# Summing the squares of the first half of the tokens on TensorE instead of GpSimd

## The chip, the cores and the metric
The kernel runs on one core of one Trainium2 chip. The metric is the device time of one execution in microseconds (us). The core has engines with a queue of instructions each: TensorE (PE; its weight loads are listed as PEld), VectorE (DVE), ScalarE (ACT), GpSimd (POOL), and SyncE (SP), which here issues most of the transfers.

## The reference
The kernel is one inference step of a decoder layer for a prompt of 512 tokens and 8 samples of one token each, 520 tokens of width 1024. The layer is

```
x += W_out [ GatedDeltaNet heads (8 x 64) | NSA heads (8 x 64) ]( RMSNorm(x) @ W_in )
x += MemCrossAttn( RMSNorm(x), mem K/V )
x += relu( RMSNorm(x) @ W_up )^2 @ W_down

def rms_norm(x, gain):
    xf = x.astype(jnp.float32)
    y = xf * lax.rsqrt(jnp.mean(xf * xf, axis=-1, keepdims=True) + RMS_EPS)
    return (y * gain.astype(jnp.float32)).astype(x.dtype)
```

followed by a final norm. The change concerns the first of these norms: the mean of the squares of a token's 1024 values, for the product with W_in.

## The kernel before
**Layout.** The tokens lie feature-major: 1024 features as 8 chunks c of 128 partitions, the tokens along the free dimension. They are held in two halves, h = 0 with 256 prompt tokens and h = 1 with the other 256 and the 8 samples, 264 columns.

**Products.** W_in comes in panels of 128 columns. `load` (L243) has SP transfer a panel into one of two buffers wraw, and `split` cuts it in two parts: ScalarE casts the high part whi (L235), and VectorE subtracts it to get the low part wlo (L236). The tokens are cut in the same way in `scaled`: xh by ScalarE or VectorE in turn (L323, L321), xl by VectorE (L324). A product is then three products per chunk, whi with xh, whi with xl, wlo with xh (`mm` is L194), 24 for a panel and a half. They are added up in one of two accumulators ps_g; the narrow panel "bag" (40 columns) uses ps_m. The two accumulators take turns, so a panel's half can begin once the one two places before it has been moved out.

**The norm.** The gain goes into xh and xl, and the factor 1/rms of a token, rstd, is multiplied in when an accumulator is moved out (`times_rstd`, L328, on VectorE). rstd comes from the sum of the squares over all 1024 features. For h = 1 ScalarE squares each chunk into sq (L396), and TensorE multiplies it by a 128 x 128 matrix of ones in fp32, adding up the 8 chunks in ps_t; so the sum stands on all partitions. For h = 0 the function `ssq` has ScalarE square the first chunk into the tile ssq (L297) and the others into sq (L300), GpSimd adds them up in ssq (L301), and one product with ones follows. `rstd` then has ScalarE do Ln (L310) and Exp (L311).

**Order of the panels.** `mixers` calls for bag and k0 together, k1, the decay matrices of the DeltaNet heads (`dn_decay`: tiles P, 32 operations of 128x128 on VectorE in L767 of its first call, with transfers P<-cumd by SP), then q0, q1, `dn_mats`, ck, k2 and so on. bt is the bag's result, ready for five transposes (L226) whose results lead to beta and decay of the heads (sg, gd, cum, ct); of a panel of kind q or k, `dn_tile` makes pre and cv, the convolution acc (L725, L727), its gate sgm, the norm and qk (L745), for k also kt (L756). kv is what `cmp_tile` moves out of ck's accumulator.

**What sets the order.** The kernel is written in a framework of tiles that is started with `TILE = dict(schedule_with_timeline_sim=True)` (L19). It orders the instructions of each engine by a simulation of its own of when they could run, not by their place in the source, and each engine then executes its list in that order. A change of one instruction can so change the order elsewhere.

Of the kernel before, what the change touches and what calls it, by code (L numbers as in the profile page):

```python
# [7 lines left out]
F32 = mybir.dt.float32  # L8
# [3 lines left out]
AF = mybir.ActivationFunctionType  # L12
# [169 lines left out]
class Build:  # L182
# [173 lines left out]
    def setup(self):  # L356
        nc, I, cp = self.nc, self.I, self.cp
        nc.scalar.preload_act_table_set("natural_log_exp_and_others")
        X = self.x = self.xp.tile([128, 8, 520], F32, tag="x", name="x")
        self.xh = [X[:, :, 0:256], X[:, :, 256:520]]  # L360
        small = self.small = cp.tile([128, S_COLS], F32, name="small")
        nc.sync.dma_start(small[:], I["small"])
        nc.sync.dma_start(self.xh[0][:, 0:2, :], I["xa"][:, 0:2, :])
        bag = self.load(I["w_bag"])
        for c in range(2, 8, 2):
            nc.sync.dma_start(self.xh[0][:, c:c + 2, :], I["xa"][:, c:c + 2, :])
        k0 = self.load(I["w_in"][0])
        for c in range(0, 8, 4):
            nc.sync.dma_start(self.xh[1][:, c:c + 4, :], I["xb"][:, c:c + 4, :])
        cst = self.cst = cp.tile([128, C_CAU], F32, name="cst")  # L370
        nc.sync.dma_start(cst[:], I["consts"][:, 0:C_CAU])
        cau = self.ap.tile([128, 128], F32, tag="qp", name="cau", bufs=1)
        nc.sync.dma_start(cau[:], I["consts"][:, C_CAU:C_COLS])
        self.ident = cst[:, C_ID:C_ID + 128]
        self.ones = cp.tile([128, 128], F32, name="ones")
        nc.vector.memset(self.ones[:], 1.0)
        self.eps = cp.tile([128, 2], F32, name="eps")
        nc.vector.memset(self.eps[:, 0:1], EPS)
        nc.vector.memset(self.eps[:, 1:2], 1.0)
        self.idb = cp.tile([128, 128], BF16, name="idb")  # L380
        nc.vector.tensor_copy(self.idb[:], cst[:, C_ID:C_ID + 128])
        self.caub = cp.tile([128, 128], BF16, name="caub")
        nc.vector.tensor_copy(self.caub[:], cau[:])

        self.xn, self.r, self.early = [], [], []
        for h in range(2):
            n = HN[h]
            acc = self.tp.tile([128, 264], F32, tag="ssq", name="ssq") if h == 0 else None
            hl = self.xhl(h)
            for c in range(8):  # L390
                self.scaled(self.xh[h][:, c, :], n, 0, c, hl, nc.vector if c % 2 else None)
                if (h, c) == (0, 1):
                    self.early.append(self.parts(bag))
                if h:
                    sq = self.tp.tile([128, 264], F32, tag="sq", name="sq", bufs=2)
                    nc.scalar.activation(sq[:, :n], self.xh[h][:, c, :], AF.Square)  # L396
                    if c == 0:
                        total = self.psum("t")
                    self.mm(total[:, :n], self.ones[:], sq[:, :n], c == 0, c == 7)
                else:  # L400
                    self.ssq(acc, c, self.xh[h][:, c, :], n)
            if h == 0:
                self.early.append(self.parts(k0))
            self.r.append(self.rstd(acc, n, total if h else None))
            self.xn.append(hl)


# [1420 lines left out]
```

## Time and profile before

| | |
|---|---|
| median of 3 runs | 978.94 us (977.99 to 979.73) |
| the profiled execution | 981.79 us, of it 979.9 us span |
| TensorE busy | 945.0 us, 96% |
| VectorE busy | 695.0 us, 71% |
| ScalarE busy | 481.4 us, 49% |
| GpSimd busy | 144.3 us, 15%; 44.1 us of it in 47 additions of L301 |

The span is the time from the first to the last instruction that the profiler recorded on the core; the profiled execution's own time is a little longer. Busy shares are means over the whole program. An operation's duration overlaps that of the next one on the same engine a little, so several in a row take less than the sum of their durations. The additions of L301 are those of this norm and of later ones.

### The profile page before, as it was taken

Reading aid. Unit: us, or ns where it says so; the run is one execution under the profiler, and the core shown is the slowest. Engines: PE = TensorE matmul, PEld = TensorE weight load, DVE = VectorE, ACT = ScalarE, POOL = GpSimd, SP = SyncE. Lnnn points to the kernel's source line nnn. Section 1 sums busy time; section 2 is a strip of 40 time slices with the busy share of each in tenths; the row PEclk is TensorE's granted clock in tenths of the full one; section 3 lists DMA queues with packets and bytes.
Section 4 is the critical chain, followed back from the end, with each engine's and each line's share of the span. In section 5 each row is a group of like instructions: output and inputs, shape, how many; then the busy total and the mean of one; then the engine's idle time right before and its main releaser. Section 6 shows DMA issues by size and latency. Waiting matters only on the chain.

```text
span 979.9 us, 20589 instructions
## 1 busy us (share of the span) xinstructions
PE 945.0 (96%) x8160; PEld 870.5 (89%) x8160; DVE 695.0 (71%) x1405; ACT 481.4 (49%) x1041; POOL 144.3 (15%) x209
## 2 busy tenths in 40 slices
PE   6999999999999998999999999999999999999995
PEld 5989898898878876789988889899999999999994
DVE  6698669898777769756566569798676766666433
ACT  4485304168665444354444456576544454455331
POOL 2101008612031134104100004100000000000020
PEclk9999999999999999999999999999999999999997
DMA  7344553122033553355465532123322232233303
GB/s 271 127 162 141 165 166 113 65 66 69 24 125 117 192 199 110 139 186 198 188 235 217 216 108 87 33 98 125 112 99 98 87 109 97 88 108 108 108 12 88
DMA packets 57000, 123.78 MB, mean 126 GB/s; under 512 B 7608, under 2 KB 23672, under 8 KB 54184
## 3 DMA queue, kind: packets, MB, share of 16 engines
q1 hardware_dynamic: 54696, 113.29, 33.6%
q0 software_dynamic: 2208, 9.17, 2.6%
q8 instruction: 64, 1.05, 0.4%
q14 instruction: 32, 0.26, 0.1%
HBM read 111.06 MB, written 13.47 MB: 127 GB/s over the span
## 4 chain that ended last, share of the span: by engine, by line
PE 84%; DVE 10%; DMA 2%; ACT 2%; issue 1%; SPq 0%; POOL 0%; DVEq 0%; ACTq 0%
PE ps_g L194 37%; PE ps_o L194 14%; PE ps_m L194 11%; PE ps_t L194 11%; PE ps_s L194 8%; PE ps_t L226 2%; DVE wlo L236 1%; DMA wraw<-in_w_in 1%; DVE nb L806 1%; DMA out_mk_o<-mk 1%; PE ps_m L226 1%; DVE st L821 1%; DVE Xd L823 1%; DVE x L1625 1%; DVE kp L1159 1%
## 5 line engine op out<-in xcount | busy, mean ns | idle before, releaser
L194 PE MATMUL ps_g<-xh,whi 128*128 128x264 f32 (+1 forms) x672 | 195.1, 291 | 3.6 <-DVE nq L441 1.5
L194 PE MATMUL ps_g<-xh,wlo 128*128 128x264 f32 (+1 forms) x672 | 192.2, 287 | 1.9 <-DVE wlo L236 1.9
L194 PE MATMUL ps_g<-xl,whi 128*128 128x264 f32 (+1 forms) x672 | 194.0, 289 | 0.0
L194 PEld LDWEIGHTS ps_g<-xh,whi 128*128 128x128 f32 x672 | 127.7, 190 | 9.7 <-issue 5.1
L194 PEld LDWEIGHTS ps_g<-xh,wlo 128*128 128x128 f32 x672 | 127.5, 190 | 4.6 <-DVE wlo L236 2.3
L194 PEld LDWEIGHTS ps_g<-xl,whi 128*128 128x128 f32 x672 | 128.0, 190 | 2.6 <-issue 1.2
L301 POOL TENSOR_TENSOR ssq<-ssq,sq 128x256 f32<-128x256 f32 (+2 forms) x47 | 44.1, 938 | 513.7 <-ACT sq L300 513.4
L235 ACT CAST whi<-wraw 128x1024 fp32r<-128x1024 f32 (+1 forms) x67 | 69.4, 1037 | 95.0 <-PE ps_g L194 47.6
L235 ACT CAST wh<-wr 128x512 fp32r<-128x512 f32 x112 | 68.9, 620 | 67.4 <-PE ps_g L194 28.2
L236 DVE TENSOR_TENSOR wlo<-wraw,whi 128x1024 fp32r<-128x1024 f32 (+1 forms) x67 | 84.6, 1264 | 23.5 <-ACT whi L235 23.0
L236 DVE TENSOR_TENSOR wl<-wr,wh 128x512 fp32r<-128x512 f32 x112 | 76.3, 687 | 28.7 <-ACT wh L235 26.8
L194 PE MATMUL ps_g<-tyh,wl 128*128 128x260 f32 x256 | 72.3, 283 | 1.1 <-DVE wl L236 1.1
L194 PE MATMUL ps_g<-tyh,wh 128*128 128x260 f32 x256 | 72.6, 284 | 0.0
L194 PE MATMUL ps_g<-tyl,wh 128*128 128x260 f32 x256 | 72.5, 283 | 0.0
L194 PE MATMUL ps_o<-hh,wh 128*128 128x260 f32 x256 | 72.4, 283 | 0.0
L194 PE MATMUL ps_t<-hh,wh 128*128 128x260 f32 x256 | 72.4, 283 | 0.0
L194 PE MATMUL ps_t<-hh,wl 128*128 128x260 f32 x256 | 72.3, 283 | 0.0
L194 PE MATMUL ps_o<-hh,wl 128*128 128x260 f32 x256 | 72.3, 283 | 0.0
L194 PE MATMUL ps_o<-hl,wh 128*128 128x260 f32 x256 | 72.2, 282 | 0.0
L194 PE MATMUL ps_t<-hl,wh 128*128 128x260 f32 x256 | 72.1, 282 | 0.0
L235 ACT CAST wh<-ws 128x512 fp32r<-128x512 f32 x64 | 39.5, 617 | 48.7 <-PE ps_o L194 32.5
L236 DVE TENSOR_TENSOR wl<-ws,wh 128x512 fp32r<-128x512 f32 x64 | 43.7, 684 | 18.6 <-ACT wh L235 18.5
(466 smaller groups left out, 2539.2 us busy)
## 6 DMA issues: line engine op xcount, KB each, us to landing
wr<-in_w_up SPq DMA_DIRECT2D x64, 256.0 KB, 3.0
wr<-in_w_dn SPq DMA_DIRECT2D x64, 256.0 KB, 2.6
wraw<-in_w_in SPq DMA_DIRECT2D x26, 512.0 KB, 4.1
mK<-in_mkt SPq DMA_DIRECT2D x8, 1024.0 KB, 4.8
mK<-in_mv SPq DMA_DIRECT2D x8, 1024.0 KB, 6.9
w<-in_w SPq DMA_DIRECT2D x8, 512.0 KB, 3.5
wraw<-in_w_mk SPq DMA_DIRECT2D x8, 512.0 KB, 4.0
wraw<-in_w_mv SPq DMA_DIRECT2D x8, 512.0 KB, 3.3
```

Of the source, the lines that this page charges most:

```text
L194: self.nc.tensor.matmul(out, lhsT, rhs, start=start, stop=stop, skip_group_check=True)
L226: self.nc.tensor.transpose(out, in_, self.ident[:k, :k])
L235: self.nc.scalar.copy(hi, x)
L236: self.nc.vector.tensor_tensor(lo, x, hi.bitcast(F32), op=ALU.subtract)
L301: nc.gpsimd.tensor_tensor(acc[:, :n], acc[:, :n], sq[:, :n], op=ALU.add)
L806: nc.vector.transpose(nb[s], P[s, :, s].rearrange("p c i -> p i c"))
L821: eng.tensor_tensor(tv, nb[:, j + 1:32, j].unsqueeze(2).to_broadcast([128, n, m]), x[:, j - c0, 0:m].unsqueeze(1).to_broadcast([128, n, m] ...
L823: eng.tensor_tensor(rest, rest, tv, op=ALU.subtract)
L1159: nc.vector.tensor_tensor(t[rows, 1, :], src, t[64 * g:64 * g + 64, 0, :].bitcast(F32), op=ALU.subtract)
L1625: nc.vector.scalar_tensor_tensor(x[:, i, :], ps, self.gain(4, i), x[:, i, :], op0=ALU.mult, op1=ALU.mult)
```

## The change
The first half's squares are treated as the second half's are: each of the 8 chunks is squared into sq and multiplied by the ones, added up in ps_o for h = 0 and in ps_t for h = 1. The seven additions of GpSimd, the tile ssq and the one product with it are gone from `setup`; other users of `ssq` stay.

```diff
         for h in range(2):
             n = HN[h]
-            acc = self.tp.tile([128, 264], F32, tag="ssq", name="ssq") if h == 0 else None
             hl = self.xhl(h)
             for c in range(8):
                 self.scaled(self.xh[h][:, c, :], n, 0, c, hl, nc.vector if c % 2 else None)
                 if (h, c) == (0, 1):
                     self.early.append(self.parts(bag))
-                if h:
-                    sq = self.tp.tile([128, 264], F32, tag="sq", name="sq", bufs=2)
-                    nc.scalar.activation(sq[:, :n], self.xh[h][:, c, :], AF.Square)
-                    if c == 0:
-                        total = self.psum("t")
-                    self.mm(total[:, :n], self.ones[:], sq[:, :n], c == 0, c == 7)
-                else:
-                    self.ssq(acc, c, self.xh[h][:, c, :], n)
+                sq = self.tp.tile([128, 264], F32, tag="sq", name="sq", bufs=2)
+                nc.scalar.activation(sq[:, :n], self.xh[h][:, c, :], AF.Square)
+                if c == 0:
+                    total = self.psum("ot"[h])
+                self.mm(total[:, :n], self.ones[:], sq[:, :n], c == 0, c == 7)
             if h == 0:
                 self.early.append(self.parts(k0))
-            self.r.append(self.rstd(acc, n, total if h else None))
+            self.r.append(self.rstd(None, n, total))
             self.xn.append(hl)
```

The framework makes a new order from this for the first quarter of the program on TensorE, VectorE and ScalarE; behind about 360 us of the old profile the orders are the same. Lines behind the change have numbers lower by four in the changed kernel (L763 is the old L767).

The first place is on ScalarE, around the rstd of the second half (L310 is Ln, L311 Exp, L235 the cast of a panel's high part). Before:

```order
L396 ACTIVATE sq<-x 128x264 x4
L235 CAST whi<-wraw 128x1024
L396 ACTIVATE sq<-x 128x264 x2
L310 ACTIVATE rstd<-ps_t,eps 128x264
L311 ACTIVATE rstd<-rstd 128x264
L725 ACTIVATE acc<-pre,small 128x512
L235 CAST whi<-wraw 128x1024
```

The changed kernel, same engine and place:

```order
L394 ACTIVATE sq<-x 128x264 x3
L235 CAST whi<-wraw 128x1024
L394 ACTIVATE sq<-x 128x264 x3
L310 ACTIVATE rstd<-ps_t,eps 128x264
L235 CAST whi<-wraw 128x1024
L311 ACTIVATE rstd<-rstd 128x264
L721 ACTIVATE acc<-pre,small 128x512 x2
```

The cast of panel q1 has moved from behind a convolution step to between Ln and Exp. On VectorE the low part wlo of that panel has moved with it, to ahead of bt. Before:

```order
L236 TENSOR_TENSOR wlo<-wraw,whi 128x1024
L328 TENSOR_TENSOR pre<-ps_g,rstd 128x256
L328 TENSOR_TENSOR bt<-ps_m,rstd 40x264
L328 TENSOR_TENSOR pre<-ps_g,rstd 128x256
L328 TENSOR_TENSOR cv<-ps_g,rstd 128x8
```

The changed kernel, VectorE, same place:

```order
L236 TENSOR_TENSOR wlo<-wraw,whi 128x1024
L328 TENSOR_TENSOR pre<-ps_g,rstd 128x256
L236 TENSOR_TENSOR wlo<-wraw,whi 128x1024
L328 TENSOR_TENSOR bt<-ps_m,rstd 40x264
L328 TENSOR_TENSOR pre<-ps_g,rstd 128x256
L328 TENSOR_TENSOR cv<-ps_g,rstd 128x8
```

One wlo more stands ahead of bt. On TensorE the last product with ones of the second half (ps_t<-sq,ones) and the transposes of bt (L226) stand like this in the changed kernel, where the ps_g are the end of panel k1's second half:

```order
L194 MATMUL ps_g<-xh_162,whi 128x264
L194 MATMUL ps_g<-xl_163,whi 128x264
L194 MATMUL ps_t<-sq,ones 128x264
L194 MATMUL ps_g<-xh_162,wlo 128x264
L194 MATMUL ps_g<-xh_162,whi 128x264
L194 MATMUL ps_g<-xl_163,whi 128x264
L194 MATMUL ps_g<-xh_162,wlo 128x264
L226 MATMUL ps_t<-cst,bt 128x40 x4
L226 MATMUL ps_t<-cst,bt 8x40
```

Four products stand between them; before, the last two products with ones stood ahead of that panel's whole half, 24 products.

The last place is on VectorE, where the second half of ck is moved out (kv 128x264), the accumulator that the second half of k2 takes next. Before:

```order
L687 COPY ct<-ps_t 32x128
L727 SCALAR_TENSOR_TENSOR acc<-pre,small,acc 128x512
L328 TENSOR_TENSOR kv<-ps_g,rstd 128x264
L727 SCALAR_TENSOR_TENSOR acc<-pre,small,acc 128x512
L222 COPY G<-kv 64x256 x2
L671 COPY be<-ps_m 128x64
L236 TENSOR_TENSOR wlo<-wraw,whi 128x1024
L729 TENSOR_SCALAR sgm<-acc 128x512
L328 TENSOR_TENSOR pre<-ps_g,rstd 128x256
L767 SCALAR_TENSOR_TENSOR P<-P,cum,cst 128x128 x4
```

The changed kernel, VectorE, up to the same kv:

```order
L763 SCALAR_TENSOR_TENSOR P<-P,cum,cst 128x128 x4
L723 SCALAR_TENSOR_TENSOR acc<-pre,small,acc 128x512
L727 TENSOR_TENSOR acc<-acc,sgm 128x512
L763 SCALAR_TENSOR_TENSOR P<-P,cum,cst 128x128 x5
L741 SCALAR_TENSOR_TENSOR qk_260<-acc,sgm 128x2x128
L741 SCALAR_TENSOR_TENSOR qk_261<-acc,sgm 128x2x128
L752 TENSOR_TENSOR kt<-ps_m,ex 128x4x128
L763 SCALAR_TENSOR_TENSOR P<-P,cum,cst 128x128 x4
L723 SCALAR_TENSOR_TENSOR acc<-pre,small,acc 128x512
L763 SCALAR_TENSOR_TENSOR P<-P,cum,cst 128x128 x7
L752 TENSOR_TENSOR kt<-ps_m,ex 128x4x128
L328 TENSOR_TENSOR kv<-ps_g,rstd 128x264
```

This kv has moved from ahead of the 32 P operations to behind all of them.

## Rows read from the trace of the kernel before

**Rows 1.** Six windows of 20 us from 20 to 140 us: sum and mean
```profile
sum 120.00, PE 120.00 PEld 109.30 DVE 85.99 ACT 59.24 POOL 10.06; mean PE 20.00 PEld 18.22 DVE 14.33 ACT 9.87 POOL 1.68
```

**Rows 2.** Waits of TensorE, 0 to 20 us: total, times, longest
```profile
PE ps_m L194 <- ACT whi L235: 6.3, 1, 6.3
...
PE ps_m L194 <- DVE xl L324: 1.0, 2, 0.8
```

**Rows 3.** Timeline of GpSimd, 4 to 15 us: start, duration, instruction, count
```profile
8.36 3.27 POOL L301 TENSOR_TENSOR ssq<-ssq,sq 128x256 f32<-128x256 f32 x4 [1.62 <-ACT sq L300]
11.79 1.60 POOL L301 TENSOR_TENSOR ssq<-ssq,sq 128x256 f32<-128x256 f32 x2 [0.16 <-ACT sq L300]
```

**Rows 4.** Timeline of VectorE, 4 to 15 us
```profile
8.06 0.48 DVE L324 SCALAR_TENSOR_TENSOR xl<-x,small,xh 128x256 fp32r<-128x256 f32 x1
...
10.89 3.18 DVE L324 SCALAR_TENSOR_TENSOR xl<-x,small,xh 128x256 fp32r<-128x256 f32 x4
```

**Rows 5.** Chain of waits, 14 to 60 us: start, time, group, count
```profile
22.35 0.89 PE ps_t L194 x4
...
31.55 2.89 PE ps_g L194 x24
34.45 0.40 PE ps_t L226 x5
...
56.67 0.86 PE ps_t L194 x2
57.53 2.53 PE ps_g L194 x21
```

**Rows 6.** Timeline of TensorE, 4 to 20 us
```profile
16.32 0.41 PE L194 MATMUL ps_g<-xh,wlo 128*128 128x256 f32 x1
16.53 0.33 PE L194 MATMUL ps_g<-xh,whi 128*128 128x256 f32 x1
```

**Rows 7.** Timeline of VectorE, 30 to 72 us
```profile
32.56 0.42 DVE L328 TENSOR_TENSOR bt<-ps_m,rstd 40x264 f32<-40x264 f32 x1 [1.66 <-ACT rstd L311]
...
36.24 1.21 DVE L236 TENSOR_TENSOR wlo<-wraw,whi 128x1024 fp32r<-128x1024 f32 x1
...
54.21 0.41 DVE L328 TENSOR_TENSOR kv<-ps_g,rstd 128x264 f32<-128x264 f32 x1
...
61.10 1.14 DVE L767 SCALAR_TENSOR_TENSOR P<-P,cum,cst 128x128 f32<-128x128 f32 x4 [1.16 <-DMA P<-cumd]
62.16 0.75 DVE L745 SCALAR_TENSOR_TENSOR qk<-acc,sgm 128x256 f32<-128x256 f32 x2
...
64.29 1.92 DVE L767 SCALAR_TENSOR_TENSOR P<-P,cum,cst 128x128 f32<-128x128 f32 x7
...
69.24 0.68 DVE L756 TENSOR_TENSOR kt<-ps_m,ex 128x512 f32<-128x512 f32 x1
```

**Rows 8.** Timeline of ScalarE, 30 to 72 us
```profile
31.59 0.48 ACT L310 ACTIVATE rstd<-ps_t,eps 128x264 f32<-128x264 f32 x1 [0.80 <-PE ps_t L194]
...
34.36 1.05 ACT L235 CAST whi<-wraw 128x1024 fp32r<-128x1024 f32 x1 [0.23 <-PE ps_g L194]
```

**Rows 9.** Window from the begin of bt to the end of kv
```profile
32.56:54.62 22.06, 22.06 (x184) 21.63 (x183) 20.09 (x56) 13.14 (x28) 3.35 (x9) 1.00 0.38 119
```

**Rows 10.** Timeline of TensorE, 366 to 376 us
```profile
370.63 0.50 PE L194 MATMUL ps_g<-wlo,xm 128*128 128x512 f32 x1 [2.58 <-DVE wlo L236]
```

**Rows 11.** Windows from 370 to 376 us (first row: the columns)
```profile
core 0: us, PE busy (x) PEld busy (x) DVE busy (x) ACT busy (x) POOL busy (x), PEclk, DMA share, GB/s
370.00:372.00 2.00, 1.37 (x5) 1.15 (x6) 2.00 (x3) 0.03 (x1) 2.00 (x2) 0.90 0.22 39
372.00:374.00 2.00, 2.00 (x6) 1.52 (x6) 2.00 (x4) 0.00 (x0) 2.00 (x2) 0.50 0.58 223
374.00:376.00 2.00, 2.00 (x19) 1.36 (x19) 2.00 (x7) 1.35 (x3) 0.92 (x1) 0.75 0.38 133
```

**Rows 12.** Waits of TensorE, 140 to 380 us
```profile
PE ps_g L194 <- DVE wlo L236: 3.3, 2, 2.6
PE ps_g L194 <- DVE nq L441: 1.5, 2, 1.2
```

## The prediction
> **What bounds the kernel now.** I read the share of busy time by engine first, then the windows, then what TensorE waits for, and last the chain of waits through the part of the program that the change puts in another order. From 20 to 140 us TensorE is busy in 120.00 of 120.00 us, while VectorE has 85.99 us of work there and ScalarE 59.24 [rows 1]. So this stretch is worth what TensorE issues in it, and an engine beside it costs nothing as long as its result is there in time. In the first 20 us TensorE waits 6.3 us for the first cast weights and 1.0 us for the low parts xl of the tokens [rows 2]. The question is therefore double: what changes in the first 20 us, and whether VectorE stays early enough once the order is another.
>
> **The start.** The seven additions on GpSimd go. They take 0.8 us each [rows 3]. Beside them VectorE's xl operations take 0.80 us (3.18 for four), where one that began just before them took 0.48 [rows 4]. With the additions gone I put the last xl about 3 us earlier. In exchange TensorE gets eight products with ones for the first half instead of one. Such a product is two passes in the trace, and four passes took 0.89 us [rows 5], so each is 0.445 us at the full clock: 7 x 0.445 = 3.1 us. At the lower of its two clock levels (1.2 GHz) I take twice that. Four of the eight fall into the time in which TensorE still waits for weights and xl, the others among the products of the first panels.
>
> What decides here is the clock. Before, one 256-column product followed another by 0.21 us until 16.53 us, at the level of 1.2 GHz [rows 6]; afterwards 24 products of 264 columns took 2.89 us, 0.12 us each, the level of 2.4 GHz [rows 5]. In the changed kernel TensorE begins with two products with ones before the weights are there and has work from then on with smaller gaps. Counted by hand from these pitches, the end of the first panel's first half comes 2.2 us earlier if the clock rises at about 10 us, 0.9 us earlier at 12, 0.3 us later at 14.6 and 1.4 us later if it rises at 16.5 as before. I take -0.9, as TensorE's gaps become fewer, and keep -2.2 to +1.4.
>
> The Trainium skill, TensorE: Matmul & The Clock Gate, section "What's actually happening", says that the throttled state is the default and that activity releases it. By that rule the products with ones, put ahead of the first panel, would bring the rise forward; the sum by it would be the -2.2 end. The trace of before agrees only so far that the rise came after TensorE's work had closed up.
>
> **The second half's rstd.** Nothing in the source asks for this, but the order is made anew. On TensorE the last of the second half's eight products with ones stood ahead of all 24 products of panel k1's second half. Now it stands 20 rows into them, and only four are behind it before TensorE wants the transposes of bt. On ScalarE the cast of the next panel (whi) now stands between the Ln and the Exp of rstd, and on VectorE the wlo that follows from that cast stands ahead of bt. Before, bt began 1.01 us after the products with ones (32.56 against 31.55 [rows 5, 7]). Now the way is Ln 0.51 (0.48 [rows 8] and the hand-over), cast 1.05 [rows 8], wlo 1.14 (1.21 in the row, less the overlap with the next [rows 7]): 2.74 with 0.04 for the hand-over. bt is thus 1.73 us later against the products with ones, and what covered it, 24 products of 2.89 us in all [rows 5], is down to four, 0.48 us. TensorE's transposes wait for about 2.6 us, and the products behind them with them.
>
> **VectorE's queue ahead of kv.** This is the large term. Panel k2's second half uses an accumulator that is free once VectorE has moved out the second half of ck (kv, 128x264). Before, kv stood ahead of every one of the 32 P operations of the decay matrices, began at 54.21 and ended at 54.62 [rows 7]; k2's second half began at about 57.5 [rows 5]: 2.9 us in hand. Now all 32 P operations, four qk and two kt stand ahead of kv. From the begin of bt to the end of kv VectorE had 20.09 us of work in 22.06 us [rows 9]. To the work come
> - 32 P at 1.14 / 4 less the overlap, 0.263 (1.92 us for seven [rows 7] is 0.27): 8.4 us
> - four qk, 0.75 us for two less the overlap [rows 7], 0.335 each: 1.3 us
> - two kt at 0.60 (0.68 less the overlap [rows 7]): 1.2 us
> - two more 512-wide ones, taken as kt, and one small, 0.2: 1.4 us
> - and one wlo goes: -1.1 us.
>
> Together +11.2, so 31.3 us of work. Into this go waits for the cast of ck and for the second transfer of P, the like of which was 1.16 us before [rows 7]. Idle time was 2.0 us in the old stretch; I take 1.4, and keep 0 to 2.4. So bt to kv lasts 32.7 us instead of 22.06, 10.6 us longer, and with the 1.7 us of the later bt VectorE's way from the products with ones to kv grows by 12.4.
>
> TensorE's own way from there to k2's second half hardly grows: 20 products now stand before it (-2.4 us), but two products for norms, 0.86 us each [rows 5], and eight transposes of about 0.1 us (five narrower ones took 0.40 [rows 5]) are added in between: +0.2 with all. The loss is 12.4 - 2.9 (what was in hand) - 0.2 = 9.3 us, of which 2.6 us show at bt, perhaps 5 us just before k2's second half and the rest at small waits between. With the idle bounds: 7.9 to 10.3. Of what is queued behind the waiting instruction: TensorE takes its products in order, so the whole rest of the program moves by this sum. Not counted is what VectorE is ahead by later, since its P operations are then done.
>
> **The clock after the wait.** Before, TensorE waited 2.58 us at 370.63, and in the window from 372 the granted clock was 0.50, the 1.2 GHz level [rows 10, 11]. While that lasts a product takes twice its time; by the three windows from 370 to 376 that is 2 x 0.10 + 2 x 0.50 + 2 x 0.25 = 1.7 us. A wait of 5 us in mid-program should bring the same once, after k2's second half; before that place a slow TensorE costs nothing, as VectorE is the late one. I take 1.5, with 0 to 1.7.
>
> **Later.** Up to about 360 us rows are in another order, and then they are the same. TensorE's waits for VectorE from 140 to 380 us were 3.3 for wlo and 1.5 for nq [rows 12]; by a shift of some us they can go or grow. I found no other place where a result is as short of time as bt and kv, take nothing and keep 2 us on both sides. The library instruction of GpSimd moves from the first addition to a place near 92 us, where no one waits for GpSimd: nothing.
>
> **The sum.** -0.9 + 9.3 + 1.5 = +9.9 us. The profiled execution of before took 981.79 us (span 979.9 and 1.9 around it), so this one would be 991.7. It lay 2.85 us above the median of the runs, 978.94; against the median the forecast is 988.8, say 989. The ends: -2.2 + 7.9 + 0 - 2 = +3.7 (982.6) and 1.4 + 10.3 + 1.7 + 2 = +15.4 (994.3); all of these together on one side are unlikely, so the likeliest case has its own range from 985 to 993.
>
> **Rivals.**
> 1. The order on the chip costs less than counted. VectorE's lead of 2.9 us and the waits inside the old stretch absorb the queue, and only TensorE's seven more products count: +3.1 us, or 982. For it speaks that VectorE had 85.99 us of work in 120 [rows 1], so on the average it is not short. Against it: the 32 P stand in one block in front of kv, and a queue can't be averaged. Chance 0.10.
> 2. It is not slower, as the loss is given back. TensorE's waits for VectorE from 140 to 380 us, 3.3 and 1.5 [rows 12], and the 1.7 us of low clock behind the longest of them [rows 11] are 6.5 us. If TensorE comes there some 9 us later and VectorE does not, VectorE has its results ready and all of this goes. With the start's better end and the stalls' lower one: -2.2 + 7.9 + 0 - 6.5 = -0.8, or 978.1; with the central ones +3.4. It decides at the wlo for which TensorE waited at 370.63: with no wait there this case holds. For it speaks that VectorE has the P operations behind it earlier in TensorE's order. Against it: VectorE's results come from TensorE's products, so what is late on the one is late on the other, and beyond 360 us the order is the old one. Chance 0.05.
> 3. More than one drop of the clock. If both the wait at bt and the one before k2's second half bring the lower level, and the later waits for wlo grow as well, 1.7 us is paid two or three times and the later part adds its 2: 994 to 996. Chance 0.07. For it: one wait of 2.58 us was enough in the row [rows 10], and that at bt is as long. Against it: what is lost ahead of kv is hidden behind VectorE.
>
> The same section of the Trainium skill has an engine without work fall back to the low clock, which speaks for rival 3; by it the sum would be 1.7 us more than my forecast, 990.5. The trace shows this after the one long wait alone.
>
> **How the numbers follow.** Forecast 0.78, rivals 0.10, 0.05 and 0.07. Two in a thousand, 2 us, is about what can be told from no change here. Faster by more than that is the low end of rival 2 and what I have not thought of, 0.04; within it lie the rest of rival 2 and a little of rival 1, 0.05; slower is the rest, 0.91. The range takes the likeliest case's own and goes down to rival 1's neighbourhood: 982.5 to 993.
>
> **What would show it.** In the profile after, TensorE's waits should list bt with about 2.6 us near 30 us and kv or what frees it with about 5 us near 60 us, and VectorE should be busy without a gap through the 32 P just before. The window behind it should have a granted clock near 0.5 to 0.75 for about 3 us. At the start xl should take 0.48, with no GpSimd addition beside it, and the first 256-column products with a pitch of 0.12 should appear before 16.5 us. The forecast is wrong if kv is there in time or if TensorE makes up the loss where it used to wait for wlo and nq.

## The result and the profile after

The changed kernel takes 994.66 us (median of 5 runs, 992.12 to 994.85), the kernel before 979.73 beside it (5 runs, 977.99 to 981.66). The ratio is 1.0143 with the interval 1.0125 to 1.016: 1.4% slower. The forecast was 989.0 with the range 982.5 to 993, so the sign was right, and the size was outside the range. The profiled executions differ less: 992.17 against 981.79, +10.4 us, where the working had +9.9.

The page after shows that the loss is not in the sums. Engine, busy time, share of the span, instructions:

```profile
PE 948.1 (96%) x8174; PEld 874.5 (88%) x8174; DVE 694.1 (70%) x1405; ACT 483.0 (49%) x1041; POOL 139.9 (14%) x202
```

TensorE is busy for 3.1 us more, as much as the seven products were put at. VectorE and GpSimd have a little less than before, ScalarE 1.6 us more. The span grew by 10.5 us, from 979.9 to 990.4. TensorE's waits say where. Before, there were none from 20 to 140 us [rows 1]; after, from 20 to 140 us (what waits, for whom, us in total, times, longest):

```profile
PE ps_t L194 <- ACT sgm L731: 2.3, 1, 2.3
PE ps_t L226 <- DVE bt L328: 2.2, 1, 2.2
PE ps_g L194 <- DVE kv L328: 1.4, 1, 1.4
PE ps_t L194 <- DVE gd L630: 1.0, 1, 1.0
```

That is 6.9 us. From 140 to 200 us:

```profile
PE ps_m L226 <- DVE kv L328: 2.6, 2, 2.2
PE ps_g L194 <- DVE wlo L236: 2.1, 1, 2.1
PE ps_g L194 <- DVE Xd L819: 1.6, 1, 1.6
```

That is 6.3 us, where the kernel before has 2.8 (nq 1.5 as in [rows 12], wlo 0.7 and kv 0.6). So from 20 to 200 us TensorE waits for 13.2 us instead of 2.8, 10.4 us more. That this equals the distance of the profiled pair is chance: the waits leave out the seven products, the slow stretches shown below and what changed at the start. Behind that the waits are alike: the wait of 2.6 us for wlo of [rows 10] is 2.5 in the changed kernel.

**The first two places, in the main as forecast.** VectorE's timeline of the changed kernel, to be read against [rows 7] (start, duration, instruction, count):

```profile
35.02 0.42 DVE L328 TENSOR_TENSOR bt<-ps_m,rstd 40x264 f32<-40x264 f32 x1
...
65.64 1.93 DVE L763 SCALAR_TENSOR_TENSOR P<-P,cum,cst 128x128 f32<-128x128 f32 x7
...
68.07 0.43 DVE L328 TENSOR_TENSOR kv<-ps_g,rstd 128x264 f32<-128x264 f32 x1
```

From the begin of bt to the end of kv VectorE needs 33.5 us; it was 22.06 [rows 9], and 32.7 were forecast. TensorE's timeline of the changed kernel:

```profile
35.49 0.35 PE L226 MATMUL ps_t<-cst,bt 40*128 40x40 f32 x3 [2.22 <-DVE bt L328]
...
64.55 1.79 PE L194 MATMUL ps_t<-sgm,cst 128*128 128x512 f32 x2 [2.26 <-ACT sgm L731]
...
68.56 0.59 PE L194 MATMUL ps_g<-xh,whi 128*128 128x264 f32 x1 [1.37 <-DVE kv L328]
```

The second half of panel k2 begins at 68.56, where it was 57.53 [rows 5]: 11.0 us later. Just before it TensorE has not one wait of 5 us, as the forecast had it, but two, and slow products between. The first of the two is not VectorE's. ScalarE's timeline has the square of sgm (L731) behind a cast that waited for a panel:

```profile
62.41 1.05 ACT L235 CAST whi<-wraw 128x1024 fp32r<-128x1024 f32 x1 [2.96 <-DMA wraw<-in_w_in]
...
63.89 0.61 ACT L731 ACTIVATE sgm<-acc 128x512 f32<-128x512 f32 x1
```

SP's queue had issued that panel behind the transfers of P:

```profile
50.77 3.75 SPq L761 DMA_DIRECT2D P<-cumd  x8
54.62 0.66 SPq L243 DMA_DIRECT2D wraw<-in_w_in  x1
```

The windows of the changed kernel from 64 to 72 us (columns as in [rows 11]) show TensorE at the level of 1.2 GHz after the wait for sgm:

```profile
64.00:66.00 2.00, 1.45 (x2) 0.53 (x3) 2.00 (x8) 1.02 (x2) 0.10 (x1) 0.72 0.00 0
66.00:68.00 2.00, 1.20 (x5) 0.65 (x3) 2.00 (x7) 1.59 (x3) 0.00 (x0) 0.50 0.00 0
68.00:70.00 2.00, 1.44 (x6) 1.44 (x7) 2.00 (x6) 1.99 (x5) 0.58 (x1) 0.50 0.04 15
70.00:72.00 2.00, 2.00 (x12) 2.00 (x11) 1.56 (x4) 1.01 (x3) 0.00 (x0) 0.57 0.55 149
```

VectorE is busy in all of the first three windows while TensorE is not, and from 54.16 us to its kv it has no idle time in the timeline. So VectorE is the late one at kv, and the wait for sgm only takes time in which TensorE would otherwise have waited for kv: in before_neworder, below, the wait for sgm is 1.3 us and that for kv 3.4.

**A third place, which the prediction had not seen.** VectorE before, at about 140 us:

```profile
140.27 0.41 DVE L328 TENSOR_TENSOR kv<-ps_g,rstd 128x256 f32<-128x256 f32 x1
...
141.24 8.08 DVE L806 STREAM_TRANSPOSE nb<-P 32x1024 f32<-32x1024 f32 x4
```

VectorE after, the same instructions:

```profile
148.41 7.96 DVE L802 STREAM_TRANSPOSE nb<-P 32x1024 f32<-32x1024 f32 x4
156.40 0.42 DVE L328 TENSOR_TENSOR kv<-ps_g,rstd 128x256 f32<-128x256 f32 x1
```

The first half of panel sv is moved out (kv, 128x256) behind four block transposes of 2.0 us each instead of ahead of them. TensorE, which wants kv for its own transposes, waits for it and is slow afterwards, with 0.21 us from one 256-column product to the next until 160.5 us:

```profile
156.88 0.57 PE L226 MATMUL ps_m<-cst,kv 128*128 128x128 f32 x2 [2.17 <-DVE kv L328]
...
157.46 0.41 PE L194 MATMUL ps_g<-xl,whi 128*128 128x256 f32 x1
157.68 0.41 PE L194 MATMUL ps_g<-xh,wlo 128*128 128x256 f32 x1
```

**The start** is as forecast in its signs. TensorE's waits from 0 to 20 us have one row, where the kernel before had three: whi and xl [rows 2], and 1.2 us for wlo between them. xl on VectorE takes 0.42 us where [rows 4] had 0.80, and the pitch of TensorE's 256-column products is 0.12 from about 10.4 us, where it was 0.21 until 16.53 [rows 6]. Waits, then VectorE, then TensorE of the changed kernel:

```profile
PE ps_o L194 <- ACT sq L394: 5.8, 1, 5.8
```

```profile
9.74 1.27 DVE L324 SCALAR_TENSOR_TENSOR xl<-x,small,xh 128x256 fp32r<-128x256 f32 x3
```

```profile
10.43 0.28 PE L194 MATMUL ps_m<-xh,whi 128*40 128x256 f32 x1
10.54 0.28 PE L194 MATMUL ps_m<-xl,whi 128*40 128x256 f32 x1
```

The Trainium skill, SBUF — State Buffer, section "Summary: rules for kernel authors", has VectorE and GpSimd hold each other up when a VectorE instruction reads two inputs in SBUF and a GpSimd one reads SBUF too. xl reads two, and it took 0.80 beside additions of 0.80 and 0.42 without them, so the traces agree.

### The profile page after: what moved, and what is told of

It reads as the page before. It is cut to its first block, busy times and chain, and to the rows that moved or that the text cites. A ratio compares the mean times of both kernels' runs of the same rounds, so it can differ in the third digit from the quotient of the medians.

```text
span 990.4 us, 20605 instructions
## 1 busy us (share of the span) xinstructions
PE 948.1 (96%) x8174; PEld 874.5 (88%) x8174; DVE 694.1 (70%) x1405; ACT 483.0 (49%) x1041; POOL 139.9 (14%) x202
## 4 chain that ended last, share of the span: by engine, by line
PE 81%; DVE 9%; DMA 2%; issue 2%; ACT 1%; SPq 1%; POOL 0%; DVEq 0%; ACTq 0%
PE ps_g L194 36%; PE ps_o L194 14%; PE ps_m L194 10%; PE ps_t L194 10%; PE ps_s L194 8%; PE ps_t L226 2%; DVE wlo L236 1%; DVE P L763 1%; PE ps_m L226 1%; DVE nb L802 1%; DMA out_mk_o<-mk 1%; SPq L516 1%; DVE Xd L819 1%; DVE x L1621 1%; DVE st L817 1%
## 5 line engine op out<-in xcount | busy, mean ns | idle before, releaser
L301 POOL TENSOR_TENSOR ssq<-ssq,sq 128x256 f32<-128x256 f32 (+2 forms) x40 | 38.9, 972 | 507.0 <-ACT sq L300 507.0
L235 ACT CAST whi<-wraw 128x1024 fp32r<-128x1024 f32 (+1 forms) x67 | 69.4, 1037 | 79.5 <-PE ps_g L194 40.3
L235 ACT CAST wh<-wr 128x512 fp32r<-128x512 f32 x112 | 68.9, 621 | 67.7 <-PE ps_g L194 27.7
L235 ACT CAST wh<-ws 128x512 fp32r<-128x512 f32 x64 | 39.5, 618 | 47.3 <-PE ps_o L194 32.9
```

Source lines behind the costliest of these rows:

```text
L235: self.nc.scalar.copy(hi, x)
L301: nc.gpsimd.tensor_tensor(acc[:, :n], acc[:, :n], sq[:, :n], op=ALU.add)
```

## The experiments

The kernels below are the changed kernel or the one before with the order of every engine's instructions written out. A table has each engine's instructions by their places in the source, and each is bound to the one ahead of it; the edits are to this table.

```diff
+ORDER = {"EngineType.DVE": ...}
+def pin(tc, nc):
+    dep = mybir.DependencyInfo(mybir.DependencyClass.NoSync, mybir.DependencyReason.DATA)
+    for engine, text in ORDER.items():
...
+                if last is not None:
+                    tc.add_manual_dep(mine[k], last.name, dep, reason="order")
+                last = mine[k]
...
         Build(tc, I, O).run()
+        pin(tc, nc)
```

### The products or the order

Theory A: the loss is the new order's alone. Its rival has the products with ones cost or bring something themselves. Four kernels ran together: the two of the study once more, the change with all other instructions in the old order (after_oldorder), and the old sums on GpSimd with all other instructions in the order of the changed kernel (before_neworder).

> The kernel before once more, for the clock of each of its executions. Two accounts of why the measured distance (14.9 us) is larger than that of the two profiled executions (992.17 - 981.79 = 10.4 us). A, levels: executions of one kernel fall on levels some 2.5 us apart that differ by a stretch or two of low TensorE clock; then the fast ones here (near 978.5) show a granted clock of about 0.993 and those near 981.5 one of about 0.991. B, the profiler: the profiled execution is slower by itself; then all executions here show one clock, and their times differ without it.

> The changed kernel once more. Account A (levels of the clock): times near 992.2 with a clock of 0.986 and near 994.7 with 0.982, so 2.5 us for some 7 us more at the low level. Account B: clock and time go without each other.

> The change with the old order: the eight products with ones on TensorE, no GpSimd additions, and all other instructions of every engine held in the order of the kernel before by edges that order without a wait. My theory (the order costs, not the products): the start gains 1.7 us in the profile in spite of the 3.1 us of products, no wait at bt and none before k2's second half, so about 977 to 978, 1 to 2 us below the kernel before. Rival, the products cost their 3.1 us: 982. Rival, the change itself costs (products with ones, ps_o, squares on ScalarE): 988 or more.

> The change undone and its order kept: seven additions on GpSimd and one product with ones, all other instructions in the order of the changed kernel. My theory: everything is lost that the new order loses, 10.6 us at bt and kv with their clock and some 2 us later, and the start's gain of 1.7 us goes: 991 to 996. Rival, the change itself costs: 979 to 982.

| kernel | median, us | ratio to before (interval) |
|---|---|---|
| before_again | 980.28 | 1.0005 (0.999 to 1.002) |
| after_again | 994.52 | 1.0154 (1.0133 to 1.0174) |
| after_oldorder | 980.72 | 1.0006 (0.9992 to 1.002) |
| before_neworder | 992.85 | 1.0141 (1.0119 to 1.0163) |

The change alone does nothing that can be measured, and the order alone loses what the change loses. The waits of before_neworder from 20 to 140 us are at the same places, with the shares moved between them:

```profile
PE ps_g L194 <- DVE kv L328: 3.4, 1, 3.4
PE ps_t L226 <- DVE bt L328: 2.2, 1, 2.2
PE ps_t L194 <- ACT sgm L735: 1.3, 1, 1.3
```

after_oldorder has no wait there. It missed its expectation of 977 to 978: the gain at the start was not real. In the profiled execution of before_again the clock rises at 14.4 us, not at 16.5 as in the execution on which the prediction rests. TensorE begins the transposes of bt, behind all of this, at 34.38 us in that execution, at 32.58 in before_again and at 32.68 in after_oldorder: the earlier xl and the earlier rise pay for the 3.1 us of products, and no more.

The repeated executions of one kernel are not alike. Those of before_again go from 978.3 to 984.42 us, and the granted clock of the whole execution goes with them in the main: 978.3 at 0.994, 980.4 at 0.991, 984.42 at 0.987 (an exception is 980.18 at 0.994). So account A holds, and the profiler is not what makes an execution slow. Those of after_again go from 991.42 at 0.986 to 995.49 at 0.982. The profiled execution of the changed kernel, 992.17, was one of its quickest, and that of before one of its slower ones; hence 10.4 us between the two profiles and 14.9 between the medians.

### One move each

Each of these undoes one of the moves in the changed kernel and leaves the rest. move_kv has kv ahead of the second 16 P operations, and SP's transfer of the panel ahead of those of P:

```diff
 VectorE
+kv (128x264)
 kt
-P x16 in three groups, between kt and acc
 kt
-kv (128x264)
...
+P x16 in four groups, behind the operations on q1
 SP
+wraw<-in_w_in
 P<-cumd x8
-wraw<-in_w_in
```

move_transposes has the first half of sv moved out ahead of the block transposes:

```diff
 VectorE
+kv (128x256)
 nb<-P (STREAM_TRANSPOSE) x4
-kv (128x256)
```

move_all has both, and bt ahead of the wlo before it, with Exp of rstd ahead of the cast. after_filled leaves the order and puts ten products of constants, used nowhere, on TensorE just ahead of four of its waits (bt, sgm, the kv before k2's second half, the kv of sv), so that it is busy in them:

```diff
+    def idle(self, n, ps, before):
+        for _ in range(n):
+            self.fills.append((self.nc.tensor.matmul(ps[:], self.ones[:], self.cst[:, 0:512], start=True, stop=True, skip_group_check=True).ins, before))
```

> The changed kernel held in its own new order, with one place put back: on VectorE kv of the second half of ck stands ahead of the second 16 of the 32 P operations (these and their four exponentials on ScalarE follow in pieces), and SP issues the panel transfer ahead of P's eight. My theory: the waits of 2.3 us for sgm and of 1.4 us for kv ahead of k2's second half go and with them the stretch of low clock there, 1.6 us of loss: about 5 us less than the changed kernel, 988 to 990. Rival, VectorE has the same work and the wait only moves to the next place: 993 to 995.

> The changed kernel held in its own new order, with one place put back: on VectorE the first half of the panel sv (a kv of 128x256) is moved out ahead of the four block transposes of P, 8 us, and not behind them. My theory: this place, which the prediction did not see, costs a wait of 2.2 us and 1.7 us of low clock: about 4 us less than the changed kernel, near 990.5. Rival, the chain of VectorE behind the transposes is what sets the end and takes it back: 994.

> The changed kernel in its own new order with three places put back: bt (the cast of the next panel behind the exponential of rstd, its low part behind bt), kv with P, and the transposes. My theory: these three are the whole loss: 979 to 983. Rival, the rest of the new order or the change has a share of its own: 986 or more.

> The changed kernel held in its own new order, with ten products of constants that nothing uses on TensorE, placed where it waits: two ahead of bt's transposes, three ahead of the sgm product and three ahead of k2's second half, two ahead of the transposes of sv. The waits stay; TensorE is busy in them. Theory A, low clock behind the waits is a large part of the loss (granted clock 0.983 in the median run against 0.991): 989 to 991 with a clock of 0.989 or more. Theory B, as in my prediction one drop of 1.5 us: 993. Rival, the products cost their 8.6 us: 1000 or more.

| kernel | median, us | ratio to before (interval) |
|---|---|---|
| move_kv | 998.95 | 1.0181 (1.015 to 1.0211) |
| move_transposes | 994.7 | 1.0135 (1.0109 to 1.0161) |
| move_all | 996.64 | 1.0164 (1.0141 to 1.0188) |
| after_filled | 994.13 | 1.0132 (1.0101 to 1.0163) |

The first three missed what they were to gain.

move_kv was to gain 5 us and lost 4. The panel's transfer, put ahead of P's, waited in SP's queue for 5.7 us, by the profile for VectorE, and what stood behind it waited too. It went at 52.78 us, when VectorE had just ended a wlo (51.54 to 52.76); that it waited for its buffer is inferred from this. SP's queue, then VectorE:

```profile
52.78 0.33 SPq L243 DMA_DIRECT2D wraw<-in_w_in  x1
53.16 0.42 SPq L685 DMA_DIRECT2D cumd<-ct  x1
56.20 3.66 SPq L761 DMA_DIRECT2D P<-cumd  x8
```

```profile
59.66 1.14 DVE L763 SCALAR_TENSOR_TENSOR P<-P,cum,cst 128x128 f32<-128x128 f32 x4 [6.56 <-DMA P<-cumd]
```

P's transfers began at 56.20 instead of 50.77, VectorE stood still for 6.56 us, and TensorE then waited 5.6 us for qk. The move of kv was not tested by this; move_kv2 below does it without SP.

move_transposes moved the kv of sv's first half to 150.10, ahead of the block transposes, and the wait for it went. For the second half's kv, still behind them, TensorE waited 0.77 us, and then 3.14 us for the kv of the first half of the next panel, wv. VectorE, then TensorE:

```profile
158.77 0.42 DVE L328 TENSOR_TENSOR kv<-ps_g,rstd 128x264 f32<-128x264 f32 x1
...
166.35 0.42 DVE L328 TENSOR_TENSOR kv<-ps_g,rstd 128x256 f32<-128x256 f32 x1
```

```profile
159.25 0.44 PE L226 MATMUL ps_m<-cst,kv 128*128 128x128 f32 x2 [0.77 <-DVE kv L328]
...
166.83 0.44 PE L226 MATMUL ps_m<-cst,kv 128*128 128x128 f32 x2 [3.14 <-DVE kv L328]
```

In the new order wv's kv stands behind the operations kp; in the kernel before it stood ahead of them:

```profile
150.24 0.41 DVE L328 TENSOR_TENSOR kv<-ps_g,rstd 128x256 f32<-128x256 f32 x1
...
153.04 1.46 DVE L1159 TENSOR_TENSOR kp<-nks,kp 64x512 fp32r<-64x512 f32 x2
```

So there is a fourth place of the same kind behind the third.

move_all has move_kv's fault in it. Its third move took the wait at bt from 2.2 to 0.6 us, and that for gd, some instructions on, rose from 1.0 to 2.4:

```profile
PE ps_t L194 <- DVE gd L630: 2.4, 1, 2.4
...
PE ps_t L226 <- DVE bt L328: 0.6, 1, 0.6
```

after_filled shows what the slow stretches in the early part are worth. The products in the waits kept the clock up: in its trace no stretch is below full clock from the start's rise until 168 us. TensorE began k2's second half at 68.61 us (68.56 in the changed kernel), was about 1.1 us ahead of the changed kernel behind it, and 1.8 us ahead at 163 us. Then it waited for wv's kv, 1.90 us where the changed kernel waits 0.41. after_filled, then the changed kernel:

```profile
165.41 0.44 PE L227 MATMUL ps_m<-cst,kv 128*128 128x128 f32 x2 [1.90 <-DVE kv L334]
```

```profile
165.73 0.44 PE L226 MATMUL ps_m<-cst,kv 128*128 128x128 f32 x2 [0.41 <-DVE kv L328]
```

Of the 1.8 us 0.3 are left: where VectorE is the late one, a TensorE at full clock arrives sooner and waits longer. Behind that, from 168 to 175 us, after_filled has a slow stretch of its own that the changed kernel does not have there. The time is 0.4 us less by the medians and 0.0022 of it, 2 us, by the ratios, within both intervals, with a granted clock of the whole execution of 0.987 at the median, where the changed kernel has 0.983. The theory that the clock is the larger share of the early loss (989 to 991) falls. What the clock costs behind 168 us was not tested. The Trainium skill, TensorE: Matmul & The Clock Gate, section "What's actually happening", has activity release the clock's throttle, and the trace agrees: the granted clock from 66 to 70 us is 1.00 here and 0.50 in the changed kernel.

### The moves again, without the faults

move_kv2 leaves SP alone; instead ScalarE does the square of sgm ahead of the cast that waits for the panel. move_kvs2 moves out both halves of sv early, the second between the first and the second block transpose. move_both2 has both.

```diff
 ScalarE
+sgm<-acc (L731)
 whi<-wraw (L235)
-sgm<-acc (L731)
 VectorE
+kv (128x264)
 kt
-P x16 in three groups
 kt
-kv (128x264)
```

```diff
 VectorE
+kv (128x256)
 nb<-P (STREAM_TRANSPOSE)
+kv (128x264)
 nb<-P (STREAM_TRANSPOSE) x3
-kv (128x256)
 Xd
-kv (128x264)
```

> The changed kernel in its own new order, the place of kv put back without touching SP's queue, on which the first attempt had failed (the panel transfer put ahead there waited for its buffer and held P's eight transfers back by 6 us): on VectorE kv of ck's second half ahead of the second 16 P operations, on ScalarE the sgm square ahead of the cast that waits for the panel, the four later exponentials of P in pieces. My theory: k2's second half starts some 5 us earlier than in the changed kernel (68.6 there), and the low clock behind it goes: 988 to 990. Rival, the wait moves on along VectorE's queue: 993 to 996.

> The changed kernel in its own new order with both halves of sv moved out early: the first ahead of the four block transposes, the second behind the first of them. The first attempt put only the first half ahead, and TensorE then waited 3.3 us for the second. My theory now: VectorE had no idle time there from 149 to 175 us, so it is the bound of that stretch and most of the wait comes back a little later: 992 to 995, with the wait for kv gone from the place of the transposes. Rival, the two kv are all of it: 990.

> Both of the moves above in one kernel. If the two places are independent: the sum of the two gains, 986 to 989. If what is won at the first place is lost at the second, where VectorE is the bound: 991 or more.

| kernel | median, us | ratio to before (interval) |
|---|---|---|
| move_kv2 | 988.87 | 1.0088 (1.0056 to 1.0119) |
| move_kvs2 | 996.35 | 1.0159 (1.0132 to 1.0185) |
| move_both2 | 989.85 | 1.0099 (1.007 to 1.0128) |

move_kv2 came out as expected, 5.7 us below after_again. Both waits just before k2's second half are gone from its list of 20 to 140 us, and one of 1.4 us has come:

```profile
PE ps_t L226 <- DVE bt L328: 2.2, 1, 2.2
PE ps_o L194 <- ACT sgm L701: 1.4, 1, 1.4
PE ps_t L194 <- DVE gd L630: 1.0, 1, 1.0
```

So the block of P ahead of kv, with the square behind the cast, costs 5 to 6 us by the medians. In the trace k2's second half begins at 63.36 us, 5.2 us earlier than in the changed kernel. move_kvs2 gained nothing, and its time lies a little above the expected 992 to 995. TensorE no longer waits for either kv of sv, but 4.1 us for that of wv's first half, which VectorE begins at 165.51 us, behind kp:

```profile
165.99 0.69 PE L226 MATMUL ps_m<-cst,kv 128*128 128x128 f32 x2 [4.13 <-DVE kv L328]
```

move_both2 is no better than move_kv2, with 4.3 us at the same place. In the changed kernel VectorE is busy for 26.28 of the 27 us from 148 to 175, so what is moved forward pushes something else back that TensorE also wants. Moving sv's kv alone does not mend the third place. Whether wv's kv moved as well, or less work for VectorE ahead of it, would do so was not tried.

### Which part of the order costs what

Three kernels splice the two orders. Every engine has one order for the instructions that start before a time, and the other for the rest: new until 37.5 us, which has bt alone (new_start); new until 100 us (new_then_old); old until 100 us (old_then_new).

```diff
-ORDER = the new order of the whole program
+ORDER = the first N instructions of one order, then the rest in the sequence of the other
```

> The change with the new order for what began before 37.5 us in the changed kernel's profile (so with the wait at bt), and the old order for all that follows. My theory, a wait of 2.2 us at bt and half a microsecond around it that nothing gives back: 983 to 984. Rival, the wait at bt is only moved ahead and what follows in the old order makes it up: 980 to 981.

> The change with the new order for what began before 100 us in the changed kernel's profile (bt, sgm and kv ahead of k2's second half), and the old order from there. My theory, these places are some 9 to 10 us of the loss with their low clock: 989 to 991, and the rest of the 14 us is the later order. Rival, all of the loss is made here: 994.

> The change with the old order for what began before 100 us in the profile of the kernel before, and the new order from there (with the four block transposes ahead of both halves of sv). Theory A, the later order loses by itself: 983 to 986. Theory B, it loses only because the earlier waits have shifted the engines against one another: 980 to 981.

| kernel | median, us (range) | ratio to before (interval) | against 980.98 of before |
|---|---|---|---|
| new_start | 984.07 (981.3 to 989.06) | 1.0034 (1.0013 to 1.0056) | +3.1 |
| new_then_old | 990.86 (989.75 to 991.27) | 1.0094 (1.0073 to 1.0116) | +9.9 |
| old_then_new | 988.06 (982.92 to 991.35) | 1.0062 (1.0042 to 1.0082) | +7.1 |

new_start has the wait for bt, 2.2 us, and no other from 20 to 140 us. new_then_old has the four waits of the changed kernel there and the old list behind 140 us (kv 0.6); it is the part that the prediction worked out, and it lost 9.9 us, as much as the prediction's sum. By the interval of the ratio that is 7 to 11 us, and the sum has a gain at the start in it that was not real, so that the two agree to the decimal is luck. Its granted clock, 0.991 in the profiled execution, is that of before: apart from the end of the program it has the slow stretch at 65 us, and one later where before_again has three.

The rest comes with the order behind 100 us, in which new_then_old and the changed kernel differ. It is 3.7 us by the two medians (994.52 less 990.86), 4.5 with each against the before that ran beside it, 5.9 by the ratios. The third and the fourth place lie in it, and TensorE's waits from 140 to 200 us grew by 3.5 us (6.3 less 2.8). But these waits are not what is left at the end. At the wait for cr near 290 us TensorE has executed the same products in both kernels, and the profiled executions stand level. The changed kernel, then new_then_old:

```profile
290.49 1.11 PE L194 MATMUL ps_m<-cr,P 64*64 64x64 f32 x16 [1.28 <-DVE cr L885]
```

```profile
290.43 1.11 PE L194 MATMUL ps_m<-cr,P 64*64 64x64 f32 x16 [1.27 <-DVE cr L885]
```

The second execution of the changed kernel that was profiled, after_again, is there at 289.84. So in these executions the new order has made up by 290 us what it lost at the third and fourth place, and the 1.6 us between the spans of the first two (990.4 and 988.8) come later, where the changed kernel has slow stretches from 382 and from 406 us and new_then_old has one from 590 us. The rest of the 3.7 us lies in executions that were not profiled, with a granted clock of 0.983 at the median where new_then_old has 0.991. By the same mark move_kv2 keeps 3.3 us of the 5.2 it won (287.21).

By itself, in old_then_new, the later order costs 7.1 us, more than either theory had, and with more scatter; the parts don't add. Its mark is at 282.95, where before_again, which has the old order throughout, is at 277.87: 5.1 us, with a slow stretch from 144 to 155 us in them. Its executions again go with the clock, from 982.92 to 991.35 us, and the profiled one has a slow stretch behind cr that neither the profile after nor that of before_again has. Windows from 1.1 us behind the mark, old_then_new, then before_again:

```profile
284.00:288.00 4.00, 4.00 (x20) 2.59 (x19) 2.92 (x5) 2.15 (x6) 1.64 (x2) 0.52 0.44 128
```

```profile
279.00:283.00 4.00, 4.00 (x40) 3.02 (x40) 3.75 (x6) 1.94 (x5) 1.45 (x2) 1.00 0.43 123
```

The orders are the same there, and a wait of 1.3 us for cr stands just ahead in both. TensorE did 20 products in the window instead of 40.

No kernel of the study beat the kernel before; after_oldorder equals it.

## Why the prediction was right in sign and wrong in size

- **What bounds the kernel, and that the order decides**: right. The products count for nothing (after_oldorder, 980.72), the order for all (before_neworder, 992.85).
- **The start**, -0.9: the two parts were seen rightly, the sum is nothing (after_oldorder). The -0.9 leaned on one execution of before, whose clock rose later than in before_again.
- **The second half's rstd**, 2.6 us at bt: 2.2 in the profile, +3.1 in new_start (by its interval 1.3 to 5.5).
- **VectorE's queue ahead of kv**, 9.3 with bt: right in mechanism and about right in size, and VectorE's way of 33.5 us against 32.7 is the test of it. Where it would show was half right. Of the "perhaps 5 us just before k2's second half" 1.4 are at kv and 2.3 at sgm, and these 2.3 come from SP's queue and ScalarE, which the working did not follow past the place; but kv is late whether TensorE waits for sgm or not. move_kv2, which moves both, gains 5.7 us by the medians.
- **The clock after the wait**, +1.5 "once": too few. The profile after has slow stretches behind the waits for sgm and for the kv of sv, and two later ones. The working held that the trace shows the low clock "after the one long wait alone"; that was a misreading. The trace of before has a second stretch at 0.50, behind waits of 0.31 and 0.29 us at 394.59 and 395.26 us:

```profile
396.00:398.00 2.00, 2.00 (x7) 0.95 (x6) 2.00 (x4) 1.02 (x3) 0.76 (x1) 0.50 1.01 387
```

  What the term is worth by itself was not separated. In the early part, where VectorE is the late one, after_filled gave back next to nothing.
- **Later**, "I found no other place where a result is as short of time as bt and kv, take nothing and keep 2 us on both sides": this is the step that failed. The order behind 100 us costs 3.7 to 5.9 us more (after_again against new_then_old), beyond the 2 kept for it. There were more such places, the kv of sv behind four block transposes and that of wv behind kp, and they stood in the order of the changed kernel to be read. They show in the waits, with 3.5 us from 140 to 200 us; that they are what costs the 3.7 us is not shown, as the profiled executions are level again at 290 us. What goes with the rest is the granted clock, 0.983 against 0.991.
- **Against the median**: the sum was taken from a median of 3 runs, 978.94. The medians of before in the runs since are 979.73 to 980.98, 0.8 to 2.0 us more. With this alone the forecast is 989.8 to 991.0; the rest up to the 994.66 is what the later order costs.
- **Rivals.** The first, that the order costs less than counted, falls with new_then_old. The second, that the loss is given back later, was to be decided at the wlo of [rows 10], and the wait there stayed (2.5 us). The third, more than one drop of the clock and a later part that grows, 994 to 996, is where the time came out. It was given 0.07. Its sum doesn't come out of its own terms: with two or three drops and 2 us later, in place of the one drop, they give 992.7 to 994.4. Drops do follow more than one of the waits, and the wait for wlo from 140 to 200 us grew from 0.7 to 2.1 us; but drops kept away in the first 160 us gave little back. So the range fits, and how far its mechanism does is not shown.

What stays open: why the later order costs 3.7 us behind the new early part and 7.1 behind the old one, beyond that the clock goes with it, and why a short wait is followed by a slow stretch in some executions only.

## What to carry to other kernels

Where a framework makes the order anew, a small change is two changes; bind the old order and run it, and the two are told apart in one run. When you predict from an order, go through every place where an engine that others wait for got a long or indivisible block ahead of a result, to the end of the reordered part, and follow the queues of the transfers as well: here two places were worked out closely and two more were missed. To move one instruction forward on an engine that has no idle time pushes others back, and helps only where these are not wanted soon: kv ahead of P gained 5.7 us, the kv of sv ahead of the transposes nothing. And a list of waits does not say what is lost at the end. Compare where the engine stands at a later instruction ahead of which both orders have done the same work.

## What the runs showed of the hardware that was not expected

- One program's executions differ by up to 6 us (978.3 to 984.42 in before_again), and the granted clock of the whole execution goes with it in the main, 0.994 to 0.987; the slow stretches in the profiles lie at different places in each. For a change of a few us the profiles of two single executions say less than the medians.
- Four block transposes of 32x1024 took 8 us on VectorE, 2.0 each, against 0.42 for moving out a 128x256 accumulator. The kv that stood behind them in VectorE's order began when they were done, at 156.40 us.
